# Softmax over 16,384 rows on one core: two pairs of 4 MiB chunks loaded as 8 MiB transfers, one pair stored as one

## The chip, the core and the metric

The kernel runs on one core of one Trainium2 chip; the other cores do nothing. The metric is the device time of one launch in microseconds (us). MB and GB/s are decimal; KiB and MiB are binary.

## What is computed

A softmax with temperature 0.5 over the last axis, in float32:

```python
batch, seq, dim = 16, 1024, 512
x_scaled = x / 0.5
x_max = np.max(x_scaled, axis=-1, keepdims=True)
exp_x = np.exp(x_scaled - x_max)
return exp_x / np.sum(exp_x, axis=-1, keepdims=True)
```

The 16 x 1024 rows are independent. All of x is read once (33.55 MB) and a result of the same size is written once.

## The kernel before

**Tiling.** The 16,384 rows are cut into 8 chunks of 2,048 rows. A chunk is a tile of 128 partitions x 16 rows x 512 floats, so a partition holds 16 consecutive rows, which are 32 KiB in one piece both in DRAM and in the tile; a chunk is 4 MiB. In this text the chunks are called 1 to 8; in the code `c` counts them from 0, so chunk 3 is `c = 2`. There are 6 buffers (`BUFS`, L42), 192 KiB a partition together; chunk 7 takes the buffer of chunk 1 and chunk 8 that of chunk 2.

**Blocks.** Most chunks are one block of work. Chunk 1 is worked in three blocks (rows 0 to 3, 4 to 7 and 8 to 15 of each partition) and loaded by two transfers (rows 0 to 3: 1 MiB; rows 4 to 15: 3 MiB). Chunk 8 is worked in two blocks of 8 rows. There are 11 blocks in all (`BLOCKS`, L39).

**Work on a block.** VectorE (DVE) takes the negated maximum of each row (`shift`, L74) and doubles it (L78) to make the bias. ScalarE (ACT) computes exp(2x + bias) in place, one instruction for each of the 16 rows of a partition, and adds up the row at the same time (`exponentials`, L86). VectorE takes the reciprocals of the sums (L101) and multiplies 14 of 16 rows by them in place (`scale_vector`, L103); ScalarE multiplies the other 2 (`scale_scalar`, L112). Then the chunk is stored.

**Order.** The schedule is written out by hand, and each engine works its instructions in the order of the program:

```python
exponentials(0, rows(0)[0])
for i in range(n):
    if i + 1 < n:
        exponentials(i + 1, rows(i + 1)[0])
    scale_vector(i)
    scale_scalar(i)
    if i + 2 < n:
        shift(i + 2)
    store(i)
```

So VectorE alternates between scaling block i and taking the maxima of block i + 2. ScalarE does the exponentials of block i + 1, then its share of the scaling of block i, then issues the store of block i.

**Queues.** All loads are issued by SyncE (SP), whose queue holds nothing else (`load`, L66; called by `shift` when a block's chunk has not been loaded yet). The loads of chunks 1 to 6 wait for nothing and are issued at the start; those of chunks 7 and 8 wait until the store of the chunk that had the buffer has landed. All stores are issued from ScalarE's queue (`store`, L120).

Of the kernel before, what the change touches and what calls it, by code (L numbers as in the profile page):

```python
# [1 line left out]

# [4 lines left out]


@with_exitstack
def kernel(  # L10
    ctx: ExitStack,
    tc: tile.TileContext,
    x: bass.AP,
    out: bass.AP,
):
    nc = tc.nc
    fp32 = mybir.dt.float32
    P = nc.NUM_PARTITIONS
    AX = mybir.AxisListType.X
    EXP = mybir.ActivationFunctionType.Exp  # L20
    COPY = mybir.ActivationFunctionType.Copy
    MAX = mybir.AluOpType.max

    D = x.shape[-1]
    xf = x.flatten_outer_dims()
    of = out.flatten_outer_dims()
    N = xf.shape[0]

    G = 16
    C = N // (P * G)
    assert C * P * G == N
    xr = xf.rearrange("(c p g) d -> c p g d", p=P, g=G)
    outr = of.rearrange("(c p g) d -> c p g d", p=P, g=G)
    WHOLE = [(0, G)]
    LOADS = [[(0, 4), (4, G)]] + [WHOLE] * 7
    BLOCKS = [[(0, 4), (4, 8), (8, G)]] + [WHOLE] * 6 + [[(0, 8), (8, G)]]  # L39
    STORES = [WHOLE] * 8  # L40
    BMAX = 16
    BUFS = 6  # L42

    data = ctx.enter_context(tc.tile_pool(name="data", bufs=BUFS))
    stats = ctx.enter_context(tc.tile_pool(name="stats", bufs=6))

    ctx.enter_context(tc.manual_schedule())


    warm = stats.tile([P, 1], fp32, name="warm", bufs=1)  # L50
    nc.vector.memset(warm, 0.0)  # L51
    nc.scalar.activation(out=warm, in_=warm, func=EXP)  # L52

    chunks = {}
    blocks = [(c, lo, hi) for c in range(C) for lo, hi in BLOCKS[c]]
    n = len(blocks)
    biases, sums, recips = {}, {}, {}

    def load(c):
        if c < BUFS:  # L60
            chunks[c] = data.tile([P, G, D], fp32, name="xt")
        else:
            chunks[c] = chunks[c - BUFS]
        xt = chunks[c]
        for lo, hi in LOADS[c]:
            nc.sync.dma_start(out=xt[:, lo:hi, :], in_=xr[c][:, lo:hi, :])  # L66

    def shift(i):
        c, lo, hi = blocks[i]
        if c not in chunks:  # L70
            load(c)
        b = hi - lo
        negmax = stats.tile([P, BMAX], fp32, name="negmax")
        nc.vector.tensor_reduce(  # L74
            negmax[:, 0:b], chunks[c][:, lo:hi, :], axis=AX, op=MAX, negate=True
        )
        biases[i] = stats.tile([P, BMAX], fp32, name="bias")
        nc.vector.tensor_scalar_mul(biases[i][:, 0:b], negmax[:, 0:b], 2.0)  # L78

    def exponentials(i, rows):  # L80
        c, lo, hi = blocks[i]
        if i not in sums:
            sums[i] = stats.tile([P, BMAX], fp32, name="sums")
        for g in rows:
            row = chunks[c][:, lo + g, :]
            nc.scalar.activation(  # L86
                out=row,
                in_=row,
                func=EXP,
                bias=biases[i][:, g : g + 1],  # L90
                scale=2.0,
                accum_out=sums[i][:, g : g + 1],
            )


    def scale_vector(i):
        c, lo, hi = blocks[i]
        b = hi - lo
        k = b - b // 8
        recips[i] = stats.tile([P, BMAX], fp32, name="recip")  # L100
        nc.vector.reciprocal(recips[i][:, 0:b], sums[i][:, 0:b])  # L101
        rows = chunks[c][:, lo : lo + k, :]
        nc.vector.tensor_mul(  # L103
            rows, rows, recips[i][:, 0:k].unsqueeze(2).broadcast_to((P, k, D))
        )

    def scale_scalar(i):
        c, lo, hi = blocks[i]
        b = hi - lo
        for g in range(b - b // 8, b):  # L110
            row = chunks[c][:, lo + g, :]
            nc.scalar.activation(  # L112
                out=row, in_=row, func=COPY, scale=recips[i][:, g : g + 1]
            )

    def store(i):
        c, _, end = blocks[i]
        for lo, hi in STORES[c]:
            if hi == end:
                nc.scalar.dma_start(  # L120
                    out=outr[c][:, lo:hi, :], in_=chunks[c][:, lo:hi, :]
                )

    shift(0)
    shift(1)

    def rows(i):
        c, lo, hi = blocks[i]
        cut = hi - lo - (2 if c == 1 else 0)
        return range(cut), range(cut, hi - lo)  # L130
# [11 lines that stand above are left out]
            exponentials(i + 1, rows(i + 1)[1])  # L142


# [1 line left out]
_INS = ['x']  # L146
_OUTS = [((16, 1024, 512), 'float32')]


# [23 lines left out]
```

## Time and profile before

| what | before |
|---|---|
| time, median of 3 runs (lowest to highest) | 162.3 us (162.19 to 162.3) |
| time of the profiled execution | 162.04 us |
| its span, first to last instruction | 160.3 us |
| what lies around the span | 1.7 us |
| VectorE busy | 134.6 us (84%), 45 instructions |
| ScalarE busy | 102.2 us (64%), 273 instructions |
| moved by DMA | 67.13 MB, mean 419 GB/s over the span |
| issues | 9 loads, 8 stores |

How to read it: busy time is that of instructions at work; waits and the issuing of DMAs are not in it. Two things are close to full for nearly the whole span, VectorE and the 16 DMA engines, so the share of busy time alone doesn't tell which of them sets the end; the chain of work that ended last and the times at which transfers land have to be read as well. A time to landing runs from the issue of a transfer until its completion is seen. Instruction times in the text are counted from the start of the span.

### The profile page before, as it was taken

How to read it: one execution, taken by the hardware profiler on the slowest of the kernel's cores; microseconds unless marked ns; L12 is line 12 of the kernel's file. 1: busy time of each engine (PE TensorE's matmuls, PEld its weight loads, DVE VectorE, ACT ScalarE, POOL GpSimd, SP SyncE). 2: the span in 40 equal slices, each digit the busy share in tenths (PEclk: the TensorE clock that was granted, in tenths of full speed). 3: DMA queues.
4: the chain of work that ended last, by engine and by line, in shares of the span. 5: the costliest groups of instructions: out<-in, count | busy, mean ns of one | idle time of the engine just before them, and what ended most of it. 6: DMA issues, size and time to landing. Idle time of an engine off the chain costs nothing.

```text
span 160.3 us, 402 instructions
## 1 busy us (share of the span) xinstructions
DVE 134.6 (84%) x45; ACT 102.2 (64%) x273; POOL 0.2 (0%) x4
## 2 busy tenths in 40 slices
DVE  0607999999999999999999999999999999957000
ACT  3071549069989972998199909991899891690000
POOL 0000000000000000000000000000000000000000
DMA  5999999999999999999999999999999999999993
GB/s 180 474 409 491 409 401 483 425 393 452 458 393 401 393 425 474 409 393 499 417 393 474 442 393 468 442 393 442 474 393 417 491 401 401 491 417 401 466 442 139
DMA packets 2450, 67.13 MB, mean 419 GB/s; under 512 B 272, under 2 KB 272, under 8 KB 272
## 3 DMA queue, kind: packets, MB, share of 16 engines
q1 hardware_dynamic: 1296, 33.56, 49.4%
q10 hardware_dynamic: 1152, 33.55, 48.5%
q14 instruction: 2, 0.02, 0.0%
HBM read 33.55 MB, written 33.55 MB: 419 GB/s over the span
## 4 chain that ended last, share of the span: by engine, by line
DVE 80%; DMA 7%; ACT 4%; issue 0%; SPq 0%
DVE negmax L74 42%; DVE xt L103 36%; DMA xt<-in_x_dram 7%; ACT xt L86 4%; DVE bias L78 1%; DVE recip L101 1%; SPq L66 0%
## 5 line engine op out<-in xcount | busy, mean ns | idle before, releaser
L86 ACT ACTIVATE xt<-xt,bias 128x512 f32<-128x512 f32 x128 | 90.4, 708 | 41.5 <-DVE bias L78 40.6
L74 DVE TENSOR_REDUCE negmax<-xt 128x16 f32<-128x8192 f32 (+2 forms) x11 | 69.9, 6353 | 9.5 <-DMA xt<-in_x_dram 9.5
L103 DVE TENSOR_TENSOR xt<-xt,recip 128x7168 f32<-128x7168 f32 (+2 forms) x11 | 62.0, 5637 | 0.4
L86 ACT ACTIVATION_READ_ACCUMULATOR xt<-xt,bias 128x1 f32 x128 | 23.9, 187 | 0.0
L112 ACT ACTIVATE xt<-xt,recip 128x512 f32<-128x512 f32 x15 | 9.9, 707 | 0.0
L101 DVE RECIPROCAL recip<-sums 128x16 f32<-128x16 f32 (+2 forms) x11 | 2.4, 218 | 1.8 <-ACT xt L86 1.8
L78 DVE TENSOR_SCALAR bias<-negmax 128x16 f32<-128x16 f32 (+2 forms) x11 | 1.9, 173 | 0.4
L52 ACT ACT_TABLE_LOAD x1 | 1.3, 1283 | 0.7 <-PEq L157 0.7
L51 DVE MEMSET warm<- 128x1 f32 x1 | 0.1, 59 | 0.8 <-PEq L157 0.8
L52 ACT ACTIVATE warm<-warm 128x1 f32<-128x1 f32 x1 | 0.2, 202 | 0.0
L157 POOL MEMSET const-bfloat16-1.0<- 128x1 bf16 x1 | 0.1, 101 | 0.0
L157 POOL MEMSET const-uint8-127<- 128x1 uint8 x1 | 0.1, 101 | 0.0
L157 POOL MEMSET const-float32-0.0<- 128x1 f32 x1 | 0.1, 98 | 0.2 <-issue 0.2
L157 POOL MEMSET const-float32-1.0<- 128x1 f32 x1 | 0.1, 98 | 0.0
## 6 DMA issues: line engine op xcount, KB each, us to landing
out_dram<-xt ACTq DMA_DIRECT2D x8, 4096.0 KB, 22.8
xt<-in_x_dram SPq DMA_DIRECT2D x7, 4096.0 KB, 30.1
xt<-in_x_dram SPq DMA_DIRECT2D x1, 3072.0 KB, 11.7
xt<-in_x_dram SPq DMA_DIRECT2D x1, 1024.0 KB, 4.8
```

The lines of the kernel that those rows point to most:

```text
L51: nc.vector.memset(warm, 0.0)
L52: nc.scalar.activation(out=warm, in_=warm, func=EXP)
L74: nc.vector.tensor_reduce(negmax[:, 0:b], chunks[c][:, lo:hi, :], axis=AX, op=MAX, negate=True)
L78: nc.vector.tensor_scalar_mul(biases[i][:, 0:b], negmax[:, 0:b], 2.0)
L86: nc.scalar.activation(out=row, in_=row, func=EXP, bias=biases[i][:, g : g + 1], scale=2.0, accum_out=sums[i][:, g : g + 1],)
L101: nc.vector.reciprocal(recips[i][:, 0:b], sums[i][:, 0:b])
L103: nc.vector.tensor_mul(rows, rows, recips[i][:, 0:k].unsqueeze(2).broadcast_to((P, k, D)))
L112: nc.scalar.activation(out=row, in_=row, func=COPY, scale=recips[i][:, g : g + 1])
L157: nc = _bacc.Bacc("TRN2", target_bir_lowering=False, num_devices=1)
```

## The change

Chunks are put together in pairs: 1+2, 3+4, 5+6 and 7+8. A pair is a tile of 128 partitions x 32 rows, so that a partition holds 32 consecutive rows, 64 KiB in one piece in DRAM and in the tile. A chunk is now the first or the second half of each partition's 32 rows. There are 3 buffers for pairs, which is the same memory; pair 7+8 takes the buffer of pair 1+2.

- Loads: chunk 1 by two transfers and chunk 2 by one, as before; chunks 3+4 by one transfer of 8 MiB; chunks 5+6 by one of 8 MiB; chunks 7 and 8 by one each.
- Stores: chunks 3+4 by one transfer of 8 MiB, issued after chunk 4's last block; all others by one a chunk.
- Where a chunk is moved by itself, its pieces are still 32 KiB a partition, and in DRAM they now lie 64 KiB apart.

The blocks, their order, and every instruction on VectorE and ScalarE apart from the one store are the same.

```diff
-    xr = xf.rearrange("(c p g) d -> c p g d", p=P, g=G)
-    outr = of.rearrange("(c p g) d -> c p g d", p=P, g=G)
+    H = 2 * G
+    xr = xf.rearrange("(c p g) d -> c p g d", p=P, g=H)
+    outr = of.rearrange("(c p g) d -> c p g d", p=P, g=H)
     WHOLE = [(0, G)]
-    LOADS = [[(0, 4), (4, G)]] + [WHOLE] * 7
+    CHUNKS = [(0, G), (G, H)]
+    PAIR = [(0, H)]
+    LOADS = [[(0, 4), (4, G), (G, H)], PAIR, PAIR, CHUNKS]
     BLOCKS = [[(0, 4), (4, 8), (8, G)]] + [WHOLE] * 6 + [[(0, 8), (8, G)]]
-    STORES = [WHOLE] * 8
+    STORES = [CHUNKS, PAIR, CHUNKS, CHUNKS]
     BMAX = 16
-    BUFS = 6
+    BUFS = 3
...
-        for lo, hi in LOADS[c]:
-            nc.sync.dma_start(out=xt[:, lo:hi, :], in_=xr[c][:, lo:hi, :])
+        for lo, hi in LOADS[pair]:
+            if lo < at + G and hi > at and (pair, lo) not in loaded:
+                loaded.add((pair, lo))
+                nc.sync.dma_start(out=xt[:, lo:hi, :], in_=xr[pair][:, lo:hi, :])
+        chunks[c] = xt[:, at : at + G, :]
...
-        for lo, hi in STORES[c]:
-            if hi == end:
+        pair, at = c // 2, c % 2 * G
+        for lo, hi in STORES[pair]:
+            if hi == at + end:
                 nc.scalar.dma_start(
-                    out=outr[c][:, lo:hi, :], in_=chunks[c][:, lo:hi, :]
+                    out=outr[pair][:, lo:hi, :], in_=pairs[pair][:, lo:hi, :]
                 )
```

More of the change, by code (lines that the diff above doesn't have):

```diff
@@ L52 @@
     nc.scalar.activation(out=warm, in_=warm, func=EXP)
-    chunks = {}
+    pairs, chunks, loaded = {}, {}, set()
     blocks = [(c, lo, hi) for c in range(C) for lo, hi in BLOCKS[c]]
@@ L59, in load @@
     def load(c):
[L60 to L64, printed above, removed]
-        for lo, hi in LOADS[c]:
-            nc.sync.dma_start(out=xt[:, lo:hi, :], in_=xr[c][:, lo:hi, :])
+        pair, at = c // 2, c % 2 * G
+        if pair not in pairs:
+            if pair < BUFS:
+                pairs[pair] = data.tile([P, H, D], fp32, name="xt")
+            else:
+                pairs[pair] = pairs[pair - BUFS]
+        xt = pairs[pair]
+        for lo, hi in LOADS[pair]:
[3 more added lines that the diff above has]
+        chunks[c] = xt[:, at : at + G, :]
     def shift(i):
@@ L117, in store @@
         c, _, end = blocks[i]
-        for lo, hi in STORES[c]:
-            if hi == end:
+        pair, at = c // 2, c % 2 * G
+        for lo, hi in STORES[pair]:
+            if hi == at + end:
                 nc.scalar.dma_start(
-                    out=outr[c][:, lo:hi, :], in_=chunks[c][:, lo:hi, :]
+                    out=outr[pair][:, lo:hi, :], in_=pairs[pair][:, lo:hi, :]
                 )
```

## The prediction

> **What bounds the kernel now.** I began with the page's busy times and DMA queues.
>
> ```profile
> DVE 134.6 (84%) x45; ACT 102.2 (64%) x273; POOL 0.2 (0%) x4
> ...
> q1 hardware_dynamic: 1296, 33.56, 49.4%
> q10 hardware_dynamic: 1152, 33.55, 48.5%
> ```
>
> Loads (q1) and stores (q10) together keep the 16 DMA engines busy for 49.4 + 48.5 = 97.9% of the span. VectorE (DVE) has 84%, but the chain that ended last, in order of time, shows that its free time lies only at the two ends:
>
> ```profile
> 1.15 11.65 DMA xt<-in_x_dram
> ...
> 24.66 8.61 DVE negmax L74
> ...
> 37.49 8.61 DVE negmax L74
> ...
> 70.73 8.61 DVE negmax L74
> ...
> 137.51 5.76 ACT xt L86 x16
> ...
> 143.53 3.89 DVE xt L103
> ```
>
> From 12.8 us, when the second load has landed, VectorE goes from one instruction to the next until 147.4; its one gap is 1.8 us at the end, for the exponentials of the last block. Then only the last store is left:
>
> ```profile
> L120 ACTq DMA_DIRECT2D out_dram<-xt x1: 338/338/338, 147.5 to 147.5; - x1
> ...
> DMA to landing us min/median/max: 11.9/11.9/11.9
> ```
>
> So two resources are full at once and meet at the end. The packet records of the trace say how closely: the last packets of chunk 7's store start at 148.2, and the first of chunk 8's, issued at 147.5, at 148.4. VectorE finishing later is therefore not covered by the DMA, beyond a few tenths.
>
> **When each chunk lands and when it is needed** is what the change moves. The view of the load line, asked in short stretches around its issues, gives times to landing (each answer holds two issues: first and last number):
>
> ```profile
> DMA to landing us min/median/max: 20.9/25.5/30.1
> ...
> DMA to landing us min/median/max: 30.1/34.8/39.5
> ...
> DMA to landing us min/median/max: 53.8/63.3/72.7
> ```
>
> Issues at 1.6 (chunk 2), 2.1 (3), 2.7 (4), 3.4 (5) and 3.9 (6) make the landings 22.5, 32.2, 42.2, 57.2 and 76.6. By VectorE's timeline the maxima of chunks 2 to 6 start at 24.6, 37.4, 54.0, 70.7 and 87.3. Chunk 3 is 5.2 us early, chunk 4 11.8, chunk 5 13.4, chunk 6 10.7.
>
> **What the Trainium skill says.** (1) DMA: Bandwidth & Descriptors, "Why a DMA increments its semaphore by 16 and not by 1": only the full count of a transfer tells that data has landed; a lower count doesn't say which bytes. The trace agrees: the second block of chunk 1 (rows 4 to 7) starts at 12.82, when the whole load of rows 4 to 15 has landed. (2) Same page, "Queues, rings and completion order": each DMA engine takes turns between the queues at packet boundaries. The trace agrees: a partition's 32 KiB are one packet of 1.213 us, and with both queues at work each gets about half of the packets. (3) Same page, "Where 436 GB/s comes from": a ceiling of 435 GB/s. Here 16 x 32,768 B / 1.213 us = 432 GB/s. (4) Same page, "Latency and other measured facts": rows 512 KiB apart in DRAM gave 207 GB/s, a padded layout 214. No transfer of the trace has rows apart, so it neither agrees nor disagrees.
>
> **The change, part by part.**
>
> *Load of chunks 3+4.* Chunk 3's maxima must now wait for both. The load follows chunk 2's on a queue that no store disturbs (the first store is issued at 44.1), so it lands when chunk 4 did: 42.2, or 41.9 if I add two of the regular gaps (22.5 - 12.8 = 9.7) to 22.5. I take 42.1. VectorE reaches the instruction at 37.41, so it stalls 42.1 - 37.4 = 4.7 us (4.5 to 4.8). Behind it in VectorE's queue stand the reciprocals and scaling of chunk 2, ready from about 46, and all later maxima. ScalarE finishes its rows of chunk 2 at 45.9 and then idles until the bias of chunk 3 comes, at about 51 instead of 46.3. As VectorE has no free time up to the 1.8 us gap, and that gap moves along (its exponentials start from a VectorE result), all 4.7 us reach the last scaling: 147.4 becomes 152.1, and the last store is issued at 152.2.
>
> *Load of chunks 5+6.* Chunk 5 is needed at 70.7 + 4.7 = 75.4 and now lands with chunk 6. In the old turns that is 76.6, which would stall it by 1.2 us. But a queue with 64 KiB packets gets two thirds against 32 KiB ones. The store of chunk 1, issued at 44.1, had its first packet at 48.3, 3.2 us beyond the 1.0 that the first load took from issue to first packet; behind packets of twice the size I double that, to 51.5. By then (51.5 - 42.1) / 2.42 = 3.9 of an engine's 8 load packets are done, and the other 4.1 take turns of 2.42 + 1.21 = 3.63 us, 14.9 us together: landed at 66.4. No stall; 9 us spare. Price 0; at worst +1.2.
>
> *Loads of chunks 7 and 8* wait for the stores of chunks 1 and 2. Store 1 has 3.9 packets left at 66.4, so it lands near 71 (before: 68.1). Store 2, issued at 59.0 + 4.7 = 63.7, follows with 8 packets, partly shared with load 7, and lands near 85 (before 87.4). Load 7 is then there by about 91 and load 8 by 101; they are needed at 108.6 and 125.2. Price 0.
>
> *Store of chunks 3+4.* The issue for chunk 3 (75.6 + 4.7) goes; both go at 92.2 + 4.7 = 96.9. One issue of 0.34 us leaves ScalarE, which is not full: 0. Does the DMA run dry in the meantime? Eight loads and two stores of 9.7 us are 97 us from 1.7, to 98.7: just no. Then the pair is done at 118.1, store 5 (issued at 113.5) at 127.8; store 6 is issued only at 130.2 and runs to 140.9; store 7, issued at 137.7, ends at 150.6. So the last store, issued at 152.2, finds idle engines. The DMA loses its time there, about 6 us in two gaps; it hides nothing of VectorE's delay, and nothing of the late 3+4 store is left by then.
>
> *The last store.* On idle engines: 1.0 to the first packet, 8 x 1.213 = 9.7, 0.4 until the landing is seen = 11.1, against 11.9 with chunk 7's tail ahead of it. That gives back 0.8; engines may not start as evenly, so I take 0.5 (0 to 0.8).
>
> *Larger pieces.* Packets of 8, 24 and 32 KiB take 309, 912 and 1213 ns: 301 ns per 8 KiB and 8 ns fixed. Three 8 MiB transfers save 24 packets an engine x 8 ns = 0.2 us, of which 0.06 lies ahead of the stall. Nothing.
>
> *Rows 64 KiB apart.* Not in the trace. From 0 to the page's 3% (207 against 214): 3% of the 40 us up to the landing of 3+4, 1.2, and 0.3 of the last store: +1.5. The page's distance is 8 times larger, so I take 0.
>
> *A tile of two chunks* could add waits between its halves. The timeline shows VectorE start on rows 8 to 15 of chunk 1 at 17.64, with ScalarE still writing rows 4 to 7 of that tile until 18.2. So halves don't wait for each other: 0; if load 7 did wait for store 2 too, it and load 8 would be there by about 101, in time for both.
>
> **Sum** against the profiled execution (span 160.3, with 1.7 around it 162.04): 4.7 - 0.5 = +4.2, so 166.2. The median is 0.26 above that execution, which gives 166.5. I take 166.4.
>
> **Rivals.**
>
> - *A second stall at chunk 5.* If a 64 KiB piece is moved as two packets, turns are equal as before and 5+6 lands at 76.6: 1.2 more, 167.6. For it: no piece above 32 KiB is in the trace. Against it: three sizes up to 32 KiB, each one packet. 12%.
> - *The wider row distance slows the DMA.* Up to 166.4 + 1.5 = 167.9. For it, the page's two figures; against it, that they are for larger distances. 7%.
> - *No slower.* The DMA is 98% full, and if it alone sets the end, larger pieces help it. This decides if 3+4 lands by about 37.9 (37.4 and the half microsecond that the last store gives back): 8.39 MB between 22.5 and 37.9 is 545 GB/s. Then nothing stalls and the 0.2 us of packets is all: 161.8 to 162.3. Against it: every full chunk of the trace came at 432 GB/s. 4%.
> - *Not doing what it says:* chunks 3 and 4 still arriving by two transfers, because the load is called chunk by chunk. By the code the first call issues rows 0 to 31 and the second finds them issued. 2%, 162.3.
>
> **Chances and range.** One stall of 4.5 to 4.8 less 0 to 0.8, on 162.04 to 162.3, is 165.7 to 167.1: 75%. The range runs from 165.7 to 167.7, to take in the second stall. A difference within 0.2% (0.3 us) is about what a measurement of this kernel cannot tell from none. Slower: 75 + 12 + 7 = 94%. The no-slower case and the last one split into same 3% and faster 3%.
>
> **What would show it.** The waits should list a third wait of VectorE's L74 for the load, of about 4.7 us near 37.4; the timeline the later maxima 4.7 later and no wait at chunk 5; load packets of 64 KiB; DMA slices under 9 near 128 and 151; VectorE's busy time unchanged. It is wrong if 3+4 lands before 41, if chunk 5 waits, or if VectorE's delay shrinks on the way.

## The result and the profile after

| | before | after |
|---|---|---|
| median (lowest to highest) | 162.3 us (162.19 to 162.64) | 166.1 us (166.06 to 166.13) |
| profiled execution | 162.04 | 166.1 |
| its span | 160.3 | 164.3 |

The ratio is 1.023, with a 95% interval of 1.0216 to 1.0244: slower by 3.8 us. The forecast was 166.4, in a range of 165.7 to 167.7. Where the runs of a kernel spread, as those of some experiments below do, its ratio is made from the runs within 1.5% of its fastest.

The page of after, busy times and DMA queues:

```profile
DVE 134.7 (82%) x45; ACT 102.2 (62%) x273; POOL 0.2 (0%) x4
...
q1 hardware_dynamic: 1008, 33.55, 48.4%
q10 hardware_dynamic: 1008, 33.55, 47.4%
```

The same work takes the same busy time on both engines and the same 33.55 MB in each direction, in fewer packets. What changed is when it is done. The view of waits of after (columns: who waited for whom, us in total, times, longest):

```profile
ACT xt L94 <- DVE bias L86: 45.4, 10, 5.8
DVE negmax L82 <- DMA xt<-in_x_dram: 14.1, 3, 4.8
```

VectorE waits for loads three times instead of twice, 14.1 us instead of 9.5: 4.6 us more. ScalarE's waits for VectorE grow from 40.6 to 45.4, which is the same delay passed on. VectorE's timeline in after shows where it is (columns: start, length, instruction; in brackets the idle time before it):

```profile
33.56 3.89 DVE L111 TENSOR_TENSOR xt<-xt,recip 128x3584 f32<-128x3584 f32 x1
42.18 8.69 DVE L82 TENSOR_REDUCE negmax<-xt 128x16 f32<-128x8192 f32 x1 [4.73 <-DMA xt<-in_x_dram]
...
75.43 8.68 DVE L82 TENSOR_REDUCE negmax<-xt 128x16 f32<-128x8192 f32 x1
...
148.31 3.89 DVE L111 TENSOR_TENSOR xt<-xt,recip 128x3584 f32<-128x3584 f32 x1
```

The maxima of chunk 3 start at 42.18 and not at 37.41. Those of chunk 5 (75.43, before 70.65) have no bracket, so they waited for nothing, and the last scaling starts at 148.31, before 143.53: the delay is the same 4.8 us all the way. The last store, from the view of the store line around its issue:

```profile
L129 ACTq DMA_DIRECT2D out_dram<-xt x1: 338/338/338, 152.3 to 152.3; - x1
...
DMA to landing us min/median/max: 11.1/11.1/11.1
```

Issued 4.8 later (152.3 against 147.5), it lands in 11.1 instead of 11.9 us. 4.8 - 0.8 = 4.0, which is the difference of the two spans. Why it lands sooner is in the view of stretches of 4 us (the last two columns are the mean busy share of the DMA engines and GB/s):

```profile
124.00:128.00 4.00, 4.00 (x2) 4.00 (x12) 0.00 (x0) 1.00 0.93 401
128.00:132.00 4.00, 3.93 (x4) 3.53 (x9) 0.00 (x0) 1.00 0.67 287
...
144.00:148.00 4.00, 2.28 (x1) 4.00 (x13) 0.00 (x0) 1.00 0.91 393
148.00:152.00 4.00, 3.89 (x2) 1.27 (x3) 0.00 (x0) 1.00 0.61 262
```

Near 130 and 151 the DMA engines now have nothing to move for a part of the time, since the stores of chunks 6 and 8 come too late to follow the one ahead. By the packet records an engine stands idle for 1.4 us between 128 and 132 and for 2.6 us between 150 and 154. Before, the same stretches of the view had:

```profile
128.00:132.00 4.00, 4.00 (x1) 4.00 (x13) 0.00 (x0) 1.00 1.05 451
...
148.00:152.00 4.00, 0.00 (x0) 0.00 (x0) 0.00 (x0) 1.00 0.93 401
```

### The profile page after: what moved, and what is told of

The parts are those of the page before. It is cut to its first block, busy times and chain, and to the rows that moved or that the text cites. A ratio compares the mean times of both kernels' runs of the same rounds, so it can differ in the third digit from the quotient of the medians.

```text
span 164.3 us, 396 instructions
## 1 busy us (share of the span) xinstructions
DVE 134.7 (82%) x45; ACT 102.2 (62%) x273; POOL 0.2 (0%) x4
## 3 DMA queue, kind: packets, MB, share of 16 engines
q1 hardware_dynamic: 1008, 33.55, 48.4%
q10 hardware_dynamic: 1008, 33.55, 47.4%
HBM read 33.55 MB, written 33.55 MB: 408 GB/s over the span
## 4 chain that ended last, share of the span: by engine, by line
DVE 63%; DMA 24%; ACT 4%; SPq 1%; issue 0%
DVE negmax L82 32%; DVE xt L111 30%; DMA xt<-in_x_dram 24%; ACT xt L94 4%; DVE bias L86 1%; SPq L73 1%; DVE recip L109 1%
## 5 line engine op out<-in xcount | busy, mean ns | idle before, releaser
L94 ACT ACTIVATE xt<-xt,bias 128x512 f32<-128x512 f32 x128 | 90.4, 708 | 46.3 <-DVE bias L86 45.4
L82 DVE TENSOR_REDUCE negmax<-xt 128x16 f32<-128x8192 f32 (+2 forms) x11 | 69.9, 6354 | 14.1 <-DMA xt<-in_x_dram 14.1
```

The source lines that it names most:

```text
L82: nc.vector.tensor_reduce(negmax[:, 0:b], chunks[c][:, lo:hi, :], axis=AX, op=MAX, negate=True)
L94: nc.scalar.activation(out=row, in_=row, func=EXP, bias=biases[i][:, g : g + 1], scale=2.0, accum_out=sums[i][:, g : g + 1],)
```

## The experiments

The theory was that the whole loss is the one stall on the load of 3+4, and that the other parts (the load of 5+6, the late store, the new row distance) cost nothing. The rivals put part of it on one of these, or on the DMA. The medians of before beside the experiments were 162.22 to 162.29.

**Chunks 3 and 4 loaded apart.**

```diff
-    LOADS = [[(0, 4), (4, G), (G, H)], PAIR, PAIR, CHUNKS]
+    LOADS = [[(0, 4), (4, G), (G, H)], CHUNKS, PAIR, CHUNKS]
```

> The kernel after, with chunks 3 and 4 loaded by a transfer each; the 8 MiB load of 5+6 and the 8 MiB store of 3+4 stay. Theory (the whole loss is VectorE's one stall for the load of 3+4): VectorE's L82 waits for loads twice, not three times, 9.5 us and not 14.1, and the time is 162.2, that is 3.9 below after. Rival (the late 8 MiB store of 3+4 or the load of 5+6 costs part of it, since the DMA is full): above 163, with idle DMA slices before the last store.

Measured: median 163.23, single runs from 162.34 to 165.08; ratio to before 1.0057 (1.0036 to 1.0079). The waits, in the profiled execution of this kernel (164.98 us, one of its longest):

```profile
DVE negmax L82 <- DMA xt<-in_x_dram: 9.5, 2, 4.8
```

The third wait is gone, as expected, and 2.9 of the 3.8 us with it. But 0.9 stays, and runs of the same program differ by 2.7 us. So the theory explains most, and something else is there once the stall is not.

**The load of 3+4 alone.** Of the three 8 MiB transfers only this one:

```diff
-    LOADS = [[(0, 4), (4, G), (G, H)], PAIR, PAIR, CHUNKS]
+    LOADS = [[(0, 4), (4, G), (G, H)], PAIR, CHUNKS, CHUNKS]
-    STORES = [CHUNKS, PAIR, CHUNKS, CHUNKS]
+    STORES = [CHUNKS, CHUNKS, CHUNKS, CHUNKS]
```

> The layout of after, but of the three 8 MiB transfers only the load of 3+4. Theory: the whole loss is here, 166.1. Rival (the late store carries part of it, because the DMA has less left to do towards the end when store 3 goes early): between 163 and 165.5.

Measured: 165.92, ratio 1.0224 (1.021 to 1.0238); VectorE waits 14.0 us for loads. The one load makes 3.6 of the 3.8 us by itself. In the presence of the stall the other two transfers add 0.2, which the two intervals don't tell from nothing.

**The layout alone.**

```diff
-    LOADS = [[(0, 4), (4, G), (G, H)], PAIR, PAIR, CHUNKS]
+    LOADS = [[(0, 4), (4, G), (G, H)], CHUNKS, CHUNKS, CHUNKS]
-    STORES = [CHUNKS, PAIR, CHUNKS, CHUNKS]
+    STORES = [CHUNKS, CHUNKS, CHUNKS, CHUNKS]
```

> The layout of after (pairs of 32 rows a partition, chunks 64 KiB apart in DRAM) with no 8 MiB transfer: every chunk loaded and stored by itself. Theory: the layout costs nothing, 162.3, packets of 1.213 us as before. Rival (rows apart slow the DMA, or a tile of two chunks makes waits between its halves): up to 3% more, 163 to 167, with packets longer than 1.213 us or new waits.

Measured: 162.43, ratio 1.0007 (0.9998 to 1.0015), VectorE waits 9.4 us for loads in 2 waits, and the packets of 32 KiB take 1.213 us as before. Rows 64 KiB apart in DRAM and a tile of two chunks cost nothing that can be told from zero.

**The load of 3+4 cut after 28 rows.**

```diff
-    LOADS = [[(0, 4), (4, G), (G, H)], PAIR, PAIR, CHUNKS]
+    LOADS = [[(0, 4), (4, G), (G, H)], [(0, 28), (28, H)], PAIR, CHUNKS]
```

> The kernel after, with the load of 3+4 cut after 28 of its 32 rows (7 MiB and 1 MiB). The first part lands 2.4 us earlier than the whole, near 39.75, so that VectorE stalls 2.3 instead of 4.7. Theory (each microsecond of stall reaches the end, less what the last store gives back by finding idle DMA engines, up to 0.8): 163.5 to 163.9. Rival (the DMA's backlog covers a stall of this size): 162.5 or less. Rival (the loss is not in the stall but in having 8 MiB transfers at all): nearer 166.

Measured: 163.59, ratio 1.0086 (1.0073 to 1.0099). VectorE's timeline in this kernel:

```profile
33.76 3.89 DVE L111 TENSOR_TENSOR xt<-xt,recip 128x3584 f32<-128x3584 f32 x1
39.72 8.69 DVE L82 TENSOR_REDUCE negmax<-xt 128x16 f32<-128x8192 f32 x1 [2.06 <-DMA xt<-in_x_dram]
```

A stall of 2.06 costs 163.59 - 162.29 = 1.3 us; the full one of 4.73 cost 3.8. Between the two, 2.67 us of stall make 2.51 us of time. So the delay is passed on almost one to one, less a fixed 0.8 to 0.9 at the end, and the DMA's backlog covers no more than that.

**The load of 3+4 cut after 24 rows.**

```diff
-    LOADS = [[(0, 4), (4, G), (G, H)], PAIR, PAIR, CHUNKS]
+    LOADS = [[(0, 4), (4, G), (G, H)], [(0, 24), (24, H)], PAIR, CHUNKS]
```

> The kernel after, with the load of 3+4 cut after 24 of its 32 rows (6 MiB and 2 MiB). The first part should land near 37.3, when VectorE reaches the maxima of chunk 3 (37.4), and the second near 42.2, long before chunk 4 needs it. Theory: no stall, 162.0 to 162.4. Rival (8 MiB pairs cost something besides the stall): above 163.

Measured: 163.1, runs from 162.31 to 164.93; ratio 1.0047 (1.0029 to 1.0066). VectorE's timeline has the maxima of chunk 3 at their old time, with no wait:

```profile
33.57 3.89 DVE L111 TENSOR_TENSOR xt<-xt,recip 128x3584 f32<-128x3584 f32 x1
37.38 8.68 DVE L82 TENSOR_REDUCE negmax<-xt 128x16 f32<-128x8192 f32 x1
```

The stall is gone, as the prediction's landing times say it should be. The time is not quite what was expected: once more 0.8 us over before with a wide spread. Set against this kernel and not against before, the stall of 2.06 us adds only 0.5 (163.59 - 163.1). The two readings fit together if the time is set by whichever is later, VectorE's delayed chain or a DMA that is itself later than before.

**VectorE relieved, in after and in before.** ScalarE scales 4 instead of 2 rows of a 16-row block:

```diff
-        k = b - b // 8
+        k = b - (4 if b == 16 else b // 8)
...
-        for g in range(b - b // 8, b):
+        for g in range(b - (4 if b == 16 else b // 8), b):
```

> The kernel after, with ScalarE scaling 4 instead of 2 rows of each 16-row block, which takes 2 x 0.545 us from VectorE in each of the six blocks of 16 rows, all after the stall: 6.5 us. Theory (VectorE's chain carries the delay, and the DMA has some 5 us of idle time in after): VectorE is done by about 145.6 and the DMA, full again, sets the end near 162.0 to 162.4, although the stall of 4.7 us is still there. Rival (the delay is the DMA's, not VectorE's): stays near 166.

> The same 6.5 us taken from VectorE in the kernel before. Theory (before has VectorE and the DMA full at once): VectorE is done near 141, but the last store starts its transfer no earlier than the one ahead of it ends, and the time is 161.8 to 162.3. Rival (only VectorE sets the end before): 156 to 158.

Measured: after relieved 162.99, runs from 162.14 to 164.66, ratio to before 1.0038 (1.0023 to 1.0053), with the stall still there (14.2 us in 3 waits). Before relieved 162.28, ratio 0.9998 (0.999 to 1.0006). The last store of before relieved:

```profile
L120 ACTq DMA_DIRECT2D out_dram<-xt x1: 339/339/339, 141.7 to 141.7; - x1
...
DMA to landing us min/median/max: 17.5/17.5/17.5
```

It is issued at 141.7 instead of 147.5 and lands at 141.7 + 17.5 = 159.2, against 147.5 + 11.9 = 159.4. Of 5.8 us gained on VectorE, 0.2 reaches the end of this execution, and nothing the median. So before has two limits that end together. In after VectorE's lies later, and given 6.1 us back (the last store is issued at 146.2 instead of 152.3) the kernel falls to within 0.38% of before, with the rest still to explain.

**What is the rest?** Three kernels without a VectorE stall on the path had 0.4 to 0.6% over before. My new theory was the lateness of the store of 3+4: it takes away the DMA's reserve near 90. The next three kernels take the 8 MiB transfers one by one (the third has both loads and the relief). Of each edit only the new lines are shown.

```diff
 (the load of 5+6 alone)
+    LOADS = [[(0, 4), (4, G), (G, H)], CHUNKS, PAIR, CHUNKS]
+    STORES = [CHUNKS, CHUNKS, CHUNKS, CHUNKS]
 (the store of 3+4 alone)
+    LOADS = [[(0, 4), (4, G), (G, H)], CHUNKS, CHUNKS, CHUNKS]
+    STORES = [CHUNKS, PAIR, CHUNKS, CHUNKS]
 (after relieved, with chunks 3 and 4 stored apart)
+    STORES = [CHUNKS, CHUNKS, CHUNKS, CHUNKS]
```

> The layout of after, and of the three 8 MiB transfers only the load of 5+6. Theory now: the spread of 162.3 to 165.1 seen with chunks 3 and 4 loaded apart comes from the late store of 3+4, which leaves some DMA engines without work between about 88 and 100. Then this kernel has no such idle time and stays at 162.2 to 162.5, with a spread of a few tenths. Rival (the load of 5+6, whose larger packets crowd out the stores of chunks 1 and 2 and put the engines out of step): median near 163, spread of 2 us or more.

> The layout of after, and of the three 8 MiB transfers only the store of 3+4. Theory now (the late store takes away the DMA's reserve): median 162.7 to 163.5 with single runs up to 165, and idle DMA time between 88 and 100. Rival (the load of 5+6 is the cause): 162.2 to 162.5 with a spread of a few tenths.

> The kernel after with VectorE relieved by 6.5 us as before, and chunks 3 and 4 stored each by itself; both 8 MiB loads and the stall of 4.7 us stay. Theory now: the 0.7 us by which the relieved kernel missed came from the late store, so this one is at 162.1 to 162.4 with a spread of a few tenths. Rival (the 8 MiB loads are the cause): median near 163, spread of 2 us or more.

Measured: the load of 5+6 alone 162.64, ratio 1.0018 (1.0004 to 1.0031); the store of 3+4 alone 162.6, ratio 1.0035 (1.0021 to 1.0049), runs from 162.22 to 164.23; relieved with both loads 162.53, ratio 1.0022 (1.0012 to 1.0033). All three medians missed the ranges of the theory, by about 0.1 us, and runs differed by 1.5 us where a few tenths were expected (the load of 5+6 alone, relieved with both loads). The idle DMA time expected between 88 and 100 is not there: by the packet records of the store of 3+4 alone (an execution of 162.27 us), at least 15 of the 16 engines are at work all the time. The store has a cost of its own, clear of the layout's (1.0015 at most). For the load it is less sure: its interval overlaps that of the layout alone, though 0.18% + 0.35% is about the 0.57% of the two together, and the third kernel, with 8 MiB loads alone, is 0.22% over. Lateness can't be the cause for the load of 5+6. The next two kernels try it for the store: the kernel before, in 32 KiB pieces, with chunk 3's store held back and issued beside chunk 4's.

```diff
         for lo, hi in STORES[c]:
-            if hi == end:
-                nc.scalar.dma_start(
-                    out=outr[c][:, lo:hi, :], in_=chunks[c][:, lo:hi, :]
-                )
+            if hi == end and c != 2:
+                for d in [2, 3] if c == 3 else [c]:
+                    nc.scalar.dma_start(
+                        out=outr[d][:, lo:hi, :], in_=chunks[d][:, lo:hi, :]
+                    )
```

> The kernel before (chunks of 32 KiB a partition, every load its own), with the store of chunk 3 held back until chunk 4 is done and issued just ahead of chunk 4's: the late store without any 64 KiB piece. Theory (it is the lateness: the queue of the stores runs empty at about 87 and starts again while a load is running, with nothing in reserve): as the store of 3+4 alone, median 162.5 to 162.8, single runs above 163. Rival (the 64 KiB pieces put the engines out of step): 162.2 to 162.4 with a spread of a few tenths.

Measured: 162.29, ratio 1.0006 (1.0 to 1.0013). But ScalarE's timeline shows that the store wasn't late enough:

```profile
87.47 0.36 ACTq L121 DMA_DIRECT2D out_dram<-xt  x1
...
90.88 1.32 ACT L112 ACTIVATE xt<-xt,recip 128x512 f32<-128x512 f32 x2
92.22 0.34 ACTq L121 DMA_DIRECT2D out_dram<-xt  x1
```

The first of the two issues ran ahead of instructions that stand before it in the program (the two scalings at 90.88), as its own data was long done. The last kernel changes the order to `[3, 2]`, so that the store that has to wait comes first.

> The run before this one issued the store of chunk 3 at 87.5, when ScalarE's sequencer reached it, and not at 92.2 as the store of 3+4 is. Here chunk 4's store goes first and chunk 3's right behind it, so both start at 92.2, in 32 KiB pieces. Theory (lateness: the queue of the stores stands empty from 87 to 92 and starts again under a running load): median 162.5 to 162.8, single runs above 163, as with the store of 3+4 alone. Rival (the 64 KiB pieces): 162.2 to 162.4, spread of a few tenths.

Measured: 162.37, ratio 1.0006 (0.9995 to 1.0016), both issues from 92.13 on:

```profile
92.13 0.82 ACTq L121 DMA_DIRECT2D out_dram<-xt  x2
```

The same data, stored as late, in two transfers of 32 KiB pieces costs nothing that can be measured. So lateness alone is not the cause; it takes the single transfer of 64 KiB pieces. Whether the size of the pieces matters, or that it is one transfer instead of two, was not separated, and how it costs stays open.

The traces do say where the time goes in an execution that came out long. Here is the stretch in which the late store starts, first in the profiled execution of after relieved (163.55 us), then the same stretch in before (162.04), where no store starts late:

```profile
96.00:100.00 4.00, 3.93 (x4) 2.28 (x8) 0.00 (x0) 1.00 1.08 393
...
96.00:100.00 4.00, 3.97 (x3) 3.81 (x11) 0.00 (x0) 1.00 0.96 412
```

The DMA engines are busier and move less. The packet records show why: the store is issued at 96.1, and of the packets of the load that is running, 27 that start between 96 and 100 take 1.3 to 2.2 us instead of 1.213. That is 0.7 us for each engine. Most of the rest of the 1.3 us by which this span exceeds that of before is idle time at the end, where the last 16 packets end between 158.4 and 160.3 (158.1 and 159.1 in before). In the profiled execution of chunks 3 and 4 loaded apart (164.98) the packets between 92 and 96 lose 1.4 us for each engine. In short executions of kernels with a late store (the store of 3+4 alone, 162.27; cut after 24 rows, 162.31; both late stores in 32 KiB pieces, 162.37) they lose about 0.1 or less. So among these five the long executions are those in which the load is held up while the late store starts beside it. This is one execution of each kernel, and no kernel was made to vary it by itself.

## Why the prediction was right, point by point

- *Chunk 3 waits for the whole of 3+4*: 4.7 forecast, 4.73 measured, at the place forecast. The landing of chunk 4 in before (42.2) was the right stand-in for that of the pair.
- *All of it reaches the last store*: 152.2 forecast, 152.3 measured. The 1.8 us gap near the end moved along (1.79 at 148.07) and absorbed nothing.
- *What the last store gives back*: taken at 0.5, worked out at 0.8, measured at 0.8. This term (0.3) and the next (0.2), less 0.1 for a delay of 4.8 instead of 4.7, come near the miss of 0.3 us. The sum on idle engines, 11.1 us, was measured exactly; the caution on top of it was not needed.
- *From the profiled execution to the median*: I laid part of the 0.26 us between the two in before on top. In after the profiled execution and the median are both 166.1. That distance belonged to one execution.
- *Load of 5+6*: no stall at chunk 5, as forecast, but it landed at 2.8 + 66.9 = 69.7, not 66.4. The first packet of chunk 1's store came at 49.4, not 51.5, so the turns with the stores began earlier; the records also show load packets of up to 3.6 instead of 2.42 us just ahead of it. The step that failed here is the doubled wait for that first packet. Its base, 48.3 in before, was the first packet of one engine; on the other 15 it came between 49.1 and 49.6, so the wait hardly grew with the size of the packets ahead. The spare was 5.7 us instead of 9. The rival with a piece in two packets is out: the records have 256 load packets of 65,536 bytes, mostly of 2.418 us.
- *Loads of chunks 7 and 8*: forecast by about 91 and 101, landed at 91.5 and 104.4, with no wait of VectorE for either.
- *Rows apart*: taken at 0, measured at 1.0007 (0.9998 to 1.0015). The prediction said that the trace of before has no rows apart; chunk 1's two loads do have them (pieces of 8 and 24 KiB, 32 KiB apart in DRAM), at 309 and 912 ns a packet.
- *Late store of 3+4*: in after it is covered as said, by idle DMA time near 130 and 151. This idle time is 4.0 us, not about 6: the last packets of the store of 3+4 and of chunk 5's ended at 121.2 and 130.9 instead of 118.1 and 127.8, so the first gap is short. The step did name that cover, but not what the transfer costs without it: 0.35%, and perhaps 0.18% for the load of 5+6. The prediction's line on larger pieces ("Nothing") counted 0.2 us for them in their favour and overlooked that they can cost something where the DMA is full.
- *No slower*: this needed 3+4 to land by 37.9. Cutting the load so that chunk 3's part lands by 37.4 takes the stall away; it doesn't bring the 161.8 to 162.3 of this rival, but 163.1.

No version here beats the kernel before. With VectorE relieved it stays at 0.9998, since the DMA moves 432 GB/s by its packets for almost the whole span.

## What to carry to other kernels

Here VectorE could use a load only when all of it had landed. So before two loads are merged, set the landing of the second against the time the first is needed: here 42.2 against 37.4, and the difference is the price, less what the end of the kernel gives back. Where two resources are full and end together, a delay of one costs, while a gain on it alone can bring nothing: 4.7 us lost on VectorE cost 3.8, and 5.8 us gained on it brought none. And a part that seems free beside a stall should be timed once without it: the idle time that the stall makes can hide its price.

## What the runs showed of the hardware that I had not expected

- When the store queue starts while a load is running, its first packets come late: in before 4.2 us after the issue at 44.1 on one engine and 5.0 to 5.5 on the others, in after 5.3 to 6.0 on all, against 1.0 for the first load. The load's packets slow down in the meantime: by the records up to 2.0 us for 1.213 in before, up to 3.6 for 2.418 in after.
- In a kernel whose DMA is full, an 8 MiB store in 64 KiB pieces cost 0.35%, where the same data in two transfers of 32 KiB pieces cost nothing measurable; for an 8 MiB load it was 0.18%, barely told from zero. Runs of one program with both differed by up to 2.7 us (162.34 to 165.08), where those of before, with 32 KiB pieces, differ by 1.0 at most (162.14 to 163.16).
- An issue on ScalarE's queue can go ahead of ScalarE's instructions that come before it in the program: at 87.47 it went with four exponentials and two scalings still to start. So the order of the program held among ScalarE's own instructions, but not between them and this issue, whose data was ready.
